# Other rooms for a few tiles of a hybrid decoder block: right halves of rows for w_up's first results, the scores' tile for every fifth gate

## The chip, the cores and the metric

The kernel runs on one core of one Trainium2 chip. Its time is device microseconds (us) of one launch; the median of three runs stands for a version. The profile is of one further execution, whose own time stands beside its span below.

Engines as the profile names them: PE is TensorE (matmuls; PEld is its weight load), DVE is VectorE, ACT is ScalarE, POOL is GpSimd, SP is the engine that here issues most DMAs (SPq its queue). L12 is line 12 of the kernel before; lines of the changed kernel are one or two higher behind the edits.

## The reference, cut to what matters

One decoder block on 1024 tokens of width 1024, all in float32:

```python
proj = x @ w_in                       # -> q, f, i, og, pool_v, gate_a, gate_b
a = HGRN2(q, f, i), per-head RMSNorm, * sigmoid(og), @ w_a
b = per-group linear w_pool of (causal_mean(pool_v) - pool_v), * pool_scale
mix = (sigmoid(gate_a) * a + sigmoid(gate_b) * b) @ w_out
x = LN(alpha * x + mix)
x = LN(alpha * x + relu(x @ w_up)**2 @ w_down)
```

## The kernel before, in words

Each float32 product is three matmuls: an operand is split into a high and a low part (ACT casts the high part, L133 for activations and L279 for weights; DVE subtracts for the low part, L134 and L280), and PE adds high·high (L238), high·low (L240) and low·high (L241) in one PSUM bank. Each large product is done as seven block products of a Strassen-like scheme instead of eight. `pair` (L330 is its adding, L326 its copying out of PSUM) is one such unit: seven products p1 to p7, each of 12 matmuls of 128x512, with sums of weight blocks on DVE (L335 to L367) and three or four results that are first parked in an SBUF tile (`rooms`).

The stages, in order: proj; a recurrence over 8 heads, whose steps (`turns`) are put between proj's products; the pooling's linear `w_pool` (`pool_products`), put between the products of the last two `gates`; w_a; w_out with the first LN; w_up in 16 units of 256 columns, whose results go to DRAM; w_down; the last LN.

Two places matter here.

**The gates of w_pool.** `pool_products` makes 16 small products of six matmuls (L115 to L117) into two PSUM banks of the tag `tr`. For 14 of them a tile of the ring `f` (four rooms) is first loaded from DRAM with a sigmoid gate (SP, L929, `f<-gb`), DVE multiplies it by the product (L936), and SP writes it back to DRAM (L937, `pb<-f`). A room can be loaded again when its write has landed; a bank can be used again when DVE has read it. SP issues its DMAs in a fixed order, so a load that waits holds those behind it. The recurrence's own tile for scores, `att` (512 columns), is read last by the matmuls of L1184, before these gates begin.

**The start of w_up.** `first_normed` and `second_tokens` make the seven token operands s3, a22, s2, s1, s4 on DVE and ACT while the first three units (`pairs[0]`, `pairs[1]`, `third`) multiply with those that are ready; `run_second` writes this order down: products 3 of both pairs, the third unit's first, products 4 and 5 of both pairs, the third unit's second, products 6 and 7. A unit's results ask for tiles with `c_tile`: it takes one from the list `spare` if there is any, and else one of the rings `ca` (4 rooms), `up` (4) and `wq` (2) in the turn ca, up, ca, up, wq, counted by `n_c`. Some rooms of ca and wq are still held by the normed right halves of the tokens (`xt[1]`, four tiles, which end as the operand s4). A tile of a ring is given to the next who asks when its last reader is done; where that is late, ACT's copy out of PSUM is late, and with it the next product into that bank. The rows `r[4]` to `r[7]` (1024 columns) are normed rows of the first LN: their left halves hold the third unit's weights from then on, their right halves are transposed into the operand a22 and then idle. `spare` gets these halves and the four tiles of `xt[2]` only before `third[2:]`.

The scheduler orders instructions of different engines by priorities; the order on each engine is fixed when the kernel is built.

Of the kernel before, what the change touches and what calls it, by code (L numbers as in the profile page):

```python
# [22 lines left out]
HALF = 512  # L23
CH = HALF // P
# [29 lines left out]
def tile_hybrid_block(  # L54
# [36 lines left out]
    def nm(s):  # L91
        seq[0] += 1
        return f"{s}_{seq[0]}"
# [7 lines left out]
    def ps_tile(tag="pj", bufs=4):  # L101
        if tag == "hg":
            hg_tags.append(hg_tags.pop(0))
            tag, bufs = hg_tags[-1], 1
        return pp.tile([P, HALF], F32, tag=tag, name=nm("ps_" + tag), bufs=bufs)

    def f(t):
        return t.bitcast(F32)
# [17 lines left out]
    def split(src, tile_of):  # L126
        hi, lo = tile_of(), tile_of()
        A.copy(hi, src)
        V.tensor_sub(lo, src, f(hi))
        return hi, lo  # L130
# [32 lines left out]
    r = [None] * 8  # L163
# [4 lines left out]
    @contextmanager  # L168
    def behind_parts(name):

        with tc.issue_after(made_last[name]), tc.issue_after(made_hi[name]):
            yield
# [13 lines left out]
    xt = [[None] * CH for _ in range(3)]  # L186
# [24 lines left out]
    def second_tokens(name, *tags, normal=False):  # L211
        a11, a12, s = xt
        turned = []
        for kp in range(CH):
            if name in ("s3", "a22"):
                ps, done = transposed(r[CH:], HALF if name == "a22" else 0, kp, tags[kp % len(tags)])
                turned.append(done)
                if normal:
                    t = s[kp] if name == "s3" else half_act()
                    normed(t, ps, kp + CH * (name == "a22"))  # L220
                    ps = t
            if name == "s3":
                V.tensor_sub(s[kp], a11[kp], ps)
            elif name == "s1":
                V.tensor_add(a11[kp], s[kp], a11[kp])
            elif name == "s4":
                V.tensor_sub(a12[kp], a12[kp], s[kp])
            in_parts(name, kp, dict(s3=s, s2=s, s1=a11, s4=a12)[name][kp] if name != "a22" else ps)
            if name == "a22":
                V.tensor_sub(s[kp], ps, s[kp])  # L230
        return turned
# [51 lines left out]
    @contextmanager  # L283
    def behind_weight(n=-1):

        with tc.issue_after(hi_of[n]), tc.issue_after(lo_of[n]):
            yield
# [11 lines left out]
    n_c = [0]  # L299
# [7 lines left out]
    spare = []  # L307
# [122 lines left out]
    def run(*pairs, made=(), behind=()):  # L430

        for i, steps in enumerate(zip(*pairs)):
            made_now = list(made[i]) if made else []
            if made_now:
                made_now.pop(0)()
            with tc.issue_after(made_last[behind[i]]) if behind and behind[i] else nullcontext():
                ws = [{operand: operand() for operand in operands} for operands, _ in steps]
            for n in range(len(ws[0])):
                if made_now:
                    made_now.pop(0)()  # L440
                for w, (_, products) in zip(ws, steps):
                    operand, product = products[n]
                    product(w[operand])
                    next(turning[0], None)
# [19 lines left out]
    def run_second(pairs, third):  # L464

        def later(name, tag=None, after=None, added=False):
            def made():
                with tc.issue_after(last_add[0] if added else made_last[after]) if after else nullcontext():
                    second_tokens(name, tag, normal=True)
            return made  # L470

        made = (
            (lambda: None, later("a22", "tr")), (later("s2", after="s3"),), (later("s1", after="s2"),),
            (lambda: None, later("s4", after="s1")), (),
        )
        behind = (None, "s3", None, None, None)
        run(*(p[2 : 3] for p in pairs), made=made, behind=behind)
        with behind_parts("s3"):
            run(third[:1])
        run(*(p[3 : 5] for p in pairs), made=made[1:], behind=behind[1:])  # L480
        run(third[1:2])
        run(*(p[5 :] for p in pairs), made=made[3:], behind=behind[3:])

    def row_tile():
        return w_tile().rearrange("p k c -> p (k c)")
# [6 lines left out]
    ca = ctx.enter_context(tc.tile_pool(name="ca", bufs=4, reuse_waits="tile"))  # L492
    wq = w_scope.enter_context(tc.tile_pool(name="wq", bufs=1, side="right", reuse_waits="tile"))
# [258 lines left out]
    def loaded(src, tile_of):  # L752
        t = tile_of()
        nc.sync.dma_start(out=t, in_=src)
        return t
# [31 lines left out]
    with tc.tile_pool(name="tmp", bufs=1, side="right", reuse_waits="tile") as tmp:  # L787
# [3 lines left out]
        att = hgp.tile([P, CH, P], F32, name="att")  # L791
# [11 lines left out]
        def tt(tag, dtype=F32):  # L803
            pool = tmp if tag in ("q", "f", "og", "v") else hgp
            return pool.tile([P, HALF], dtype, tag=tag, name=nm(tag), bufs=RINGS.get(tag, 1))
# [77 lines left out]
        def pool_products():  # L883

            def ring(*tags):
                tags = list(tags)
                def tile(dtype=F32):
                    tags.append(tags.pop(0))
                    return tt(tags[-1], dtype)
                return tile  # L890

            pod_tile, w_tiles = ring("tA", "tA", "st", "st", "tH", "tH"), ring("tD", "tE", "tF", "og")

            def wide(t):
                return t.rearrange("p (k c) -> p k c", c=2 * P)

            def load(g, u):
                raw = None
                if not u:
                    raw = loaded(w_pool[g].rearrange("(k p) c -> p k c", p=P), lambda: wide(tt("tC")))  # L900
                return raw, [loaded(pod[2 * g + i][u], pod_tile) for i in range(2)]

            def parts(g, u, raw, pods):
                with behind_weight():
                    if raw is not None:
                        w_parts[g] = split(raw, lambda: wide(w_tiles(F32R)))
                    made = []
                    for t in pods:
                        hi, lo = row_tile(), row_tile()
                        pool_parts[:] = A.copy(hi, t).ins, V.tensor_sub(lo, t, f(hi)).ins  # L910
                        made.append((hi, lo))
                    return made

            w_parts = {}
            todo = [(g, u) for g in range(CH) for u in range(2)]
            soon = [load(*todo[0]), load(*todo[1])]
            pl = parts(*todo[0], *soon.pop(0))
            yield
            for n, (g, u) in enumerate(todo):
                if n + 2 < len(todo):  # L920
                    soon.append(load(*todo[n + 2]))
                wh, wl = w_parts[g]
                for i in (0, 1) if g < CH - 1 else (1, 0):
                    w = slice(i * P, (i + 1) * P)
                    j = 2 * g + i
                    final = j == KT - 1
                    t = tt("v") if final else tt("f")
                    if not final:
                        nc.sync.dma_start(out=t, in_=gbd[j][u])  # L929
                    ps = ps_tile("tr", 2)  # L930
                    mm3(ps, [(wh[:, c, w], wl[:, c, w], *pl[c]) for c in range(2)])
                    if final:
                        held[u] = t
                        A.activation(t, ps, AF.Copy, scale=pscale[:, j : j + 1])
                    else:
                        V.scalar_tensor_tensor(t, ps, pscale[:, j : j + 1], t, ALU.mult, ALU.mult)  # L936
                        nc.sync.dma_start(out=pbd[j][u], in_=t)  # L937
                    if i == (1 if g < CH - 1 else 0) and soon:
                        pl = parts(*todo[n + 1], *soon.pop(0))
                    yield  # L940
# [519 lines left out]
    r = [None] * 8  # L1460
# [39 lines left out]
    with tc.tile_pool(name="up", bufs=1, side="right", reuse_waits="tile") as up:  # L1500
        n_c[0] = 0

        def c_wide(short=None):
            n_c[0] += 1
            pool, n = ((ca, 4), (up, 4), (ca, 4), (up, 4), (wq, 2))[n_c[0] % 5]
            return pool.tile([P, HALF + 2 * HALO], F32, tag="c", name=nm("c"), bufs=n)[:, : HALO + HALF]

        def up_raw_tile():
# [52 lines left out]
            run(pairs[1][:1])  # L1561
        run_second(pairs, third)

        spare[:] = [*xt[2], *(r[t][:, HALF:] for t in range(CH, 8))]
        run(third[2:])
        spare.clear()
        rows_scope.close()
# [140 lines left out]
    for b in range(NBLK):  # L1708
# [3 lines left out]
        if last:  # L1712

            for ring in (dh, dw):
                t = fw.tile([P, M, 2, HALF], F32R, tag="draw", name=nm("dx"), bufs=2)
                ring[:0] = [(t[:, n], t[:, n + 1]) for n in (0, 2)]
        for i, (name, slot, chain, fresh, (u, nh)) in enumerate(steps):
# [13 lines left out]
            for c in range(CH):  # L1731
                t = u * CH + c
# [49 lines left out]
```

## Time and profile before

| | us |
|---|---|
| runs | 1443.65, 1442.93, 1444.0; median 1443.65 |
| profiled execution, its own time | 1443.23 |
| its span, first to last instruction | 1441.5 |
| PE busy | 1417.4 (98% of the span) |
| DVE busy | 1141.2 (79%) |
| ACT busy | 772.9 (54%) |
| POOL busy | 129.6 (9%) |

PE is busy for 98% of the span, so a change is worth what it takes from PE's waits or from PE's own work. A busy matmul is not a fast one: a 128x512 matmul starts about 0.23 us behind the one before it at the full granted clock and 0.42 us behind it at half, and both count as busy. So two views are read together: who waited for whom, and the granted clock (PEclk) stretch by stretch.

### The profile page before, as it was taken

To read this page: it belongs to the slowest core of one execution; us is meant where nothing else is said; L and a number is where in the kernel's file an instruction comes from. 1 tells how busy PE (TensorE), PEld (TensorE's weight loads), DVE (VectorE), ACT (ScalarE), POOL (GpSimd) and SP (SyncE) were. 2 spreads that over 40 slices of the span, in tenths; PEclk is the share of its full clock that TensorE was granted. 3 is DMA by queue.
4 is the path that set the end of the run, shared out by engine and by line. 5 is a ranking of instruction groups with operands and counts; after the bars stand their busy time and mean duration, and the time that the engine had idled before them with its cause. 6 is when DMAs were issued, how large, how long until landed. Compare 5 with 4: busy or idle time off the path is not lost.

```text
span 1441.5 us, 21398 instructions
## 1 busy us (share of the span) xinstructions
PE 1417.4 (98%) x7451; PEld 1172.5 (81%) x7451; DVE 1141.2 (79%) x1928; ACT 772.9 (54%) x1411; POOL 129.6 (9%) x354
## 2 busy tenths in 40 slices
PE   8999999999999999999999989999999999999997
PEld 7878888888888888878888768788888888888886
DVE  5968887897798796679996896966666887777978
ACT  5445566666656656455445664555556443433534
POOL 0023011111212110100110000100000100000000
PEclk9999999999999999999999999999999999999999
DMA  7285254444444546798762327954456874444422
GB/s 270 62 276 176 85 133 156 120 115 151 112 119 132 147 123 190 229 323 289 252 225 82 120 67 242 320 174 161 144 177 249 288 246 150 149 140 168 130 73 117
DMA packets 193036, 248.12 MB, mean 172 GB/s; under 512 B 13552, under 2 KB 112160, under 8 KB 192928
## 3 DMA queue, kind: packets, MB, share of 16 engines
q1 hardware_dynamic: 179312, 208.84, 43.7%
q0 software_dynamic: 11648, 33.56, 8.6%
q10 hardware_dynamic: 1968, 4.35, 1.0%
q8 instruction: 58, 0.95, 0.3%
q14 instruction: 50, 0.41, 0.1%
HBM read 161.24 MB, written 85.46 MB: 171 GB/s over the span
## 4 chain that ended last, share of the span: by engine, by line
PE 87%; DVE 5%; DMA 4%; ACT 2%; issue 1%; SPq 0%; DVEq 0%; ACTq 0%
PE ps_pj L238 15%; PE ps_pj L240 15%; PE ps_pj L241 15%; PE ps_pj L1661 4%; PE ps_pj L1660 4%; PE ps_pj L1659 4%; PE ps_tr L1661 2%; PE ps_tr L1660 2%; PE ps_tr L1659 2%; DMA act<-in_w_in_dram 1%; PE ps_sc L238 1%; PE ps_sc L240 1%; PE ps_sc L241 1%; PE ps_hg L241 1%; PE ps_hg L240 1%; PE ps_hg L238 1%
## 5 line engine op out<-in xcount | busy, mean ns | idle before, releaser
L238 PE MATMUL ps_pj<-act,w 128*128 128x512 f32 x1068 | 421.0, 394 | 5.6 <-ACT w L279 2.1
L240 PE MATMUL ps_pj<-act,w 128*128 128x512 f32 x1068 | 415.9, 390 | 0.0
L241 PE MATMUL ps_pj<-act,w 128*128 128x512 f32 x1068 | 414.8, 390 | 0.5 <-DVE w L280 0.5
L279 ACT CAST w<-raw 128x512 fp32r<-128x512 f32 x303 | 187.5, 621 | 237.1 <-PE ps_pj L240 169.5
L280 DVE TENSOR_TENSOR w<-raw,w 128x512 fp32r<-128x512 f32 x303 | 206.5, 685 | 78.8 <-ACT w L279 77.4
L238 PEld LDWEIGHTS ps_pj<-act,w 128*128 128x128 f32 x1068 | 200.9, 188 | 52.5 <-ACT c L326 4.2
L241 PEld LDWEIGHTS ps_pj<-act,w 128*128 128x128 f32 x1068 | 200.6, 188 | 43.6 <-DVE w L280 1.3
L240 PEld LDWEIGHTS ps_pj<-act,w 128*128 128x128 f32 x1068 | 200.8, 188 | 40.4 <-DVE act L134 0.3
L1621 ACT CAST act<-act 128x1024 fp32r<-128x1024 f32 x66 | 67.1, 1050 | 108.3 <-issue 35.0
L1622 DVE TENSOR_TENSOR act<-act,act 128x1024 fp32r<-128x1024 f32 x66 | 79.4, 1219 | 17.6 <-ACT act L1621 17.6
L1661 PE MATMUL ps_pj<-act,act 128*128 128x512 f32 x240 | 93.0, 389 | 0.0
L1660 PE MATMUL ps_pj<-act,act 128*128 128x512 f32 x240 | 93.0, 389 | 0.0
L1659 PE MATMUL ps_pj<-act,act 128*128 128x512 f32 x240 | 92.5, 389 | 0.0
L330 DVE TENSOR_TENSOR c<-c,ps_pj 128x512 f32<-128x512 f32 x91 | 62.1, 682 | 33.6 <-PE ps_pj L241 29.7
L326 ACT COPY c<-ps_pj 128x512 f32<-128x512 f32 x92 | 53.6, 582 | 7.0 <-DMA v<-c 4.8
L1660 PEld LDWEIGHTS ps_pj<-act,act 128*128 128x128 f32 x240 | 45.0, 188 | 9.4
L1661 PEld LDWEIGHTS ps_pj<-act,act 128*128 128x128 f32 x240 | 45.0, 188 | 9.3
L1659 PEld LDWEIGHTS ps_pj<-act,act 128*128 128x128 f32 x240 | 45.0, 188 | 9.3
L335 DVE TENSOR_TENSOR raw<-raw,raw 128x512 f32<-128x512 f32 x43 | 29.6, 688 | 28.2 <-DMA raw<-in_w_in_dram 17.8
L1512 ACT ACTIVATE c<-c 128x512 f32<-128x512 f32 x46 | 29.1, 632 | 30.6 <-DVE c L330 30.5
L1513 ACT ACTIVATE c<-c 128x512 f32<-128x512 f32 x61 | 38.5, 633 | 1.5
L782 POOL DMA_DIRECT2D s<-og x28 | 24.8, 1159 | 133.8 <-DVE og L1208 133.8
(496 smaller groups left out, 2756.8 us busy)
## 6 DMA issues: line engine op xcount, KB each, us to landing
h<-c SPq DMA_DIRECT2D x106, 256.0 KB, 2.9
raw<-in_w_in_dram SPq DMA_DIRECT2D x100, 256.0 KB, 3.2
act<-h SPq DMA_DIRECT2D x78, 256.0 KB, 3.0
draw<-in_w_down_dram SPq DMA_DIRECT2D x16, 1024.0 KB, 8.1
raw<-in_w_up_dram SPq DMA_DIRECT2D x56, 256.0 KB, 3.0
hf<-h SPq DMA_DIRECT2D x34, 256.0 KB, 2.9
s<-og POOLq DMA_DIRECT2D x28, 256.0 KB, 6.3
v<-v SPq DMA_DIRECT2D x16, 256.0 KB, 4.6
```

Of the source, the lines that this page charges most:

```text
L238: PE.matmul(ps, wh[:, k], th, start=first and k == 0, stop=False, skip_group_check=True)
L240: PE.matmul(ps, wh[:, k], tl, start=False, stop=False, skip_group_check=True)
L241: last_product[0] = PE.matmul(ps, wl[:, k], th, start=False, stop=k == CH - 1, skip_group_check=True).ins
L279: hi_of.append(A.copy(hi, src).ins)
L280: lo_of.append(V.tensor_sub(lo, src, f(hi)).ins)
L326: noted(A.copy(t, ps))
L330: last_add[0] = V.tensor_add(t, t, ps).ins
L1621: A.copy(hi, src)
L1622: V.tensor_sub(lo, src, f(hi))
L1659: PE.matmul(ps, hh[:, w], wh, start=fresh and n == 0, stop=False, skip_group_check=True)
L1660: PE.matmul(ps, hh[:, w], wl, start=False, stop=False, skip_group_check=True)
L1661: PE.matmul(ps, hl[:, w], wh, start=False, stop=n == M - 1, skip_group_check=True)
```

## The change

Three edits. In `run_second` the right halves of rows 4 to 7 go into `spare` as soon as products 3 of both pairs (and with them the transposes into a22) are written down, so the next four tiles asked for are r[7], r[6], r[5], r[4]; the four tiles of xt[2] are added to the list before `third[2:]`. The first six tiles of w_up come by a turn of their own, up, ca, up, up, ca, up; the fourth was wq's. And every fifth room asked for by a gate is the scores' tile `att`, so gates 5 and 10 of 16 use it.

```diff
         run(*(p[2 : 3] for p in pairs), made=made, behind=behind)
+        spare[:] = [r[t][:, HALF:] for t in range(CH, 8)]
         with behind_parts("s3"):
             run(third[:1])
...
-            w_parts = {}
+            w_parts, rooms_used = {}, [0]
...
-                    t = tt("v") if final else tt("f")
+                    rooms_used[0] += 1
+                    t = tt("v") if final else tt("f") if rooms_used[0] % 5 else att.rearrange("p c q -> p (c q)")
...
-            pool, n = ((ca, 4), (up, 4), (ca, 4), (up, 4), (wq, 2))[n_c[0] % 5]
+            pool, n = ((ca, 4), (up, 4), (ca, 4), (up, 4), (wq, 2))[n_c[0] % 5 if n_c[0] > 6 else (0, 1, 0, 1, 1, 0, 1)[n_c[0]]]
...
-        spare[:] = [*xt[2], *(r[t][:, HALF:] for t in range(CH, 8))]
+        spare.extend(xt[2])
         run(third[2:])
```

No instruction of PE, ACT or POOL is added or taken away; their order changes from the start of w_up on.

**SP among the gates of w_pool.** Names: gb4_0 is the gate of column block 4 and token half 0, pb the written product; `raw` are weights of w_a. Gates are made in the order 2_0, 3_0, 2_1, 3_1, 4_0, 5_0, 4_1, 5_1 from the fifth on. Before:

```order
L937 DMA pb2_0_1014<-f_1286_6922 128x512
L929 DMA f_1299_6982<-gb3_1_985 128x512
L754 DMA st_1333_7093<-po6_1_1007 128x512
L937 DMA pb3_0_1016<-f_1288_6933 128x512
L754 DMA st_1334_7095<-po7_1_1009 128x512
L929 DMA f_1321_7043<-gb4_0_986 128x512
L873 DMA gb6_0_990<-c_1294_6964 128x512
L253 DMA raw_1369_7282<-in_w_a_dram 128x4x128
L937 DMA pb2_1_1015<-f_1297_6971 128x512
L929 DMA f_1323_7054<-gb5_0_988 128x512
L937 DMA pb3_1_1017<-f_1299_6982 128x512
L929 DMA f_1335_7097<-gb4_1_987 128x512
```

The same place with the change:

```order
L939 DMA pb2_0_1014<-att_1067 128x512
L931 DMA f_1320_7042<-gb4_0_986 128x512
L755 DMA st_1331_7091<-po6_1_1007 128x512
L939 DMA pb3_0_1016<-f_1287_6932 128x512
L755 DMA st_1332_7093<-po7_1_1009 128x512
L931 DMA att_1067<-gb5_0_988 128x512
L874 DMA gb6_0_990<-c_1293_6963 128x512
L253 DMA raw_1367_7280<-in_w_a_dram 128x4x128
L939 DMA pb2_1_1015<-f_1296_6970 128x512
L931 DMA f_1333_7095<-gb4_1_987 128x512
L939 DMA pb3_1_1017<-f_1298_6981 128x512
L931 DMA f_1335_7106<-gb5_1_989 128x512
```

Each load stands one load earlier: where gate 8 (gb3_1) was loaded stands gate 9 (gb4_0), and so on. Gate 5 (gb2_0) is loaded into att far ahead of this, between the loads st<-po0_1 and tA<-po1_0 of SP.

**ACT and PE at the start of w_up.** ps_hg and ps_sc are the PSUM banks of products 7 and 4 of the two pairs, ps_tr banks of transposes, c and r tiles the parked results. On ACT the copy out of ps_sc stood here before, the first of these rows being the operand s4's last cast:

```order
L133 CAST act_1772_9366<-c_1671_8820 128x512
L1512 ACTIVATE c_1743_9218<-c_1743_9218 128x512
L1513 ACTIVATE c_1743_9218<-c_1743_9218 128x512
L1512 ACTIVATE c_1760_9304<-c_1760_9304 128x512
L1513 ACTIVATE c_1760_9304<-c_1760_9304 128x512
L326 COPY c_1739_9199<-ps_sc_1738_9183 128x512
```

and stands here now, two rows behind the copy out of ps_hg:

```order
L326 COPY c_1735_9179<-ps_hg_1734_9163 128x512
L279 CAST w_1745_9231<-raw_1691_8983 128x512
L326 COPY c_1737_9197<-ps_sc_1736_9181 128x512
L133 CAST act_1731_9149<-act_1730_9147 128x512
L198 ACTIVATE act_1730_9147<-ps_tr_1732_9153,prm_126 128x512
```

On PE the second pair's product 4 (12 matmuls into ps_sc) stood behind all of products 6 before:

```order
L241 MATMUL ps_pj_1707_9034<-act_1755_9281,w_1766_9345 128x512
L238 MATMUL ps_pj_1742_9205<-act_1744_9220,w_1786_9468 128x512
L240 MATMUL ps_pj_1742_9205<-act_1744_9220,w_1786_9468 128x512
L238 MATMUL ps_sc_1738_9183<-act_1728_9130,w_1750_9240 128x512
L240 MATMUL ps_sc_1738_9183<-act_1728_9130,w_1750_9240 128x512
L241 MATMUL ps_sc_1738_9183<-act_1728_9130,w_1751_9241 128x512
```

and begins now among the first pair's product 4, some 60 matmuls earlier:

```order
L238 MATMUL ps_hg_1734_9163<-act_1726_9128,w_1745_9231 128x512
L240 MATMUL ps_hg_1734_9163<-act_1726_9128,w_1745_9231 128x512
L238 MATMUL ps_sc_1736_9181<-act_1726_9128,w_1747_9237 128x512
L240 MATMUL ps_sc_1736_9181<-act_1726_9128,w_1747_9237 128x512
L241 MATMUL ps_hg_1734_9163<-act_1726_9128,w_1746_9232 128x512
L238 MATMUL ps_hg_1734_9163<-act_1728_9138,w_1745_9231 128x512
```

**DVE behind the operand s4.** Here DVE adds products out of PSUM (L330), which frees banks for the next products, and makes the low parts of s4 (L134 from c tiles). Before, the first pair's ps_pj_1707 was added behind two of the four low parts:

```order
L330 TENSOR_TENSOR c_1743_9218<-c_1743_9218,ps_tr_1764_9330 128x512
L280 TENSOR_TENSOR w_1768_9350<-raw_1723_9117,w_1767_9349 128x512
L280 TENSOR_TENSOR w_1774_9400<-raw_1696_8990,w_1773_9399 128x512
L330 TENSOR_TENSOR c_1760_9304<-c_1760_9304,ps_hg_1736_9165 128x512
L280 TENSOR_TENSOR w_1776_9404<-raw_1698_8994,w_1775_9403 128x512
L134 TENSOR_TENSOR act_1769_9354<-c_1668_8817,act_1769_9354 128x512
L134 TENSOR_TENSOR act_1770_9358<-c_1669_8818,act_1770_9358 128x512
L330 TENSOR_TENSOR c_1737_9181<-c_1737_9181,ps_pj_1707_9034 128x512
```

Now its twin, ps_pj_1705, is added behind all four and behind the sum L335, whose inputs are unit 3's loads:

```order
L330 TENSOR_TENSOR r_1624_8507<-r_1624_8507,ps_tr_1759_9325 128x512
L280 TENSOR_TENSOR w_1781_9463<-r_1620_8475,w_1780_9462 128x512
L134 TENSOR_TENSOR act_1764_9349<-c_1666_8815,act_1764_9349 128x512
L134 TENSOR_TENSOR act_1765_9353<-c_1667_8816,act_1765_9353 128x512
L134 TENSOR_TENSOR act_1766_9357<-c_1668_8817,act_1766_9357 128x512
L335 TENSOR_TENSOR raw_1795_9579<-raw_1797_9582,raw_1796_9580 128x512
L134 TENSOR_TENSOR act_1767_9361<-c_1669_8818,act_1767_9361 128x512
L330 TENSOR_TENSOR c_1735_9179<-c_1735_9179,ps_pj_1705_9032 128x512
```

## The prediction

> **What bounds the kernel.** First the page's busy times, then who waited for whom on PE, then the granted clock around the longest waits.
>
> ```profile
> span 1441.5 us, 21398 instructions
> PE 1417.4 (98%) x7451; PEld 1172.5 (81%) x7451; DVE 1141.2 (79%) x1928; ACT 772.9 (54%) x1411; POOL 129.6 (9%) x354
> ```
>
> PE is idle for 24.1 us of the span, so no change that leaves PE's work alone can bring much more. The waits of PE:
>
> ```profile
> PE ps_sc L238 <- ACT c L326: 3.2, 1, 3.2
> PE ps_pj L238 <- ACT c L326: 2.0, 3, 1.0
> PE ps_tr L115 <- DVE f L936: 2.0, 1, 2.0
> ```
>
> Two of the longest single waits are the places of this change: 3.2 us for ACT's copy out of ps_sc (start of w_up) and 2.0 us for DVE's read of a gate's bank. Stretches around both, and three wider ones used further down (us; busy time of PE, PEld, DVE, ACT, POOL with counts; granted clock, DMA share, GB/s):
>
> ```profile
> 622.20:626.00 3.80, 3.80 (x10) 2.99 (x11) 3.09 (x5) 1.76 (x3) 0.23 (x1) 0.55 0.95 319
> 852.20:857.50 5.30, 5.27 (x12) 4.13 (x13) 5.24 (x9) 1.89 (x4) 0.00 (x0) 0.50 0.27 102
> 817.60:839.30 21.70, 19.67 (x88) 14.38 (x87) 21.37 (x35) 17.64 (x32) 0.00 (x0) 1.00 0.31 94
> 839.30:857.40 18.10, 13.77 (x48) 10.25 (x47) 18.10 (x31) 12.05 (x22) 0.00 (x0) 0.83 0.22 74
> 610.00:660.00 50.00, 48.04 (x204) 39.06 (x203) 39.87 (x65) 31.16 (x56) 2.73 (x5) 0.97 1.00 335
> ```
>
> Behind each of the two waits the clock is granted at about half for 3.8 and 5.3 us, and there PE counts as busy while it works at half pace. So each wait costs nearly twice its length. The third row holds a wait of 1.10 us (832.10, below) at a clock of 1.00: what halves it lies between 1.1 and 2.0 us.
>
> [...]
>
> **Edit 1, the gates.** Ten rows of PE, DVE and SP, and the landing time of the loads:
>
> ```profile
> 608.70 0.32 SPq L929 DMA_DIRECT2D f<-gb  x1
> 613.44 0.67 SPq L937 DMA_DIRECT2D pb<-f  x1
> 615.42 0.32 SPq L929 DMA_DIRECT2D f<-gb  x1
> 615.76 0.39 PE L117 MATMUL ps_tr<-w,og 128*128 128x512 f32 x1
> 619.85 0.39 PE L117 MATMUL ps_tr<-w,tE 128*128 128x512 f32 x1
> 620.78 0.32 SPq L929 DMA_DIRECT2D f<-gb  x1
> 621.39 0.75 DVE L936 SCALAR_TENSOR_TENSOR f<-ps_tr,prm,f 128x512 f32<-128x512 f32 x1 [4.79 <-DMA f<-gb]
> 622.19 0.61 PE L115 MATMUL ps_tr<-w,tD 128*128 128x512 f32 x1 [1.96 <-DVE f L936]
> 645.63 0.68 DVE L280 TENSOR_TENSOR w<-raw,w 128x512 fp32r<-128x512 f32 x1
> 647.68 0.39 PE L241 MATMUL ps_pj<-act,w 128*128 128x512 f32 x1
> DMA to landing us min/median/max: 3.6/3.8/3.9
> ```
>
> Gate 8's product ended at 616.2, but its load, issued at 615.42, had DVE wait until 621.39; gate 10 needs gate 8's bank and began at 622.19 where its turn was 619.85 + 0.23 = 620.08. That is 2.1 us, and nine steps at half clock cost 0.2 each more: 1.7. Together 3.8.
>
> With gate 5 in att, each load moves to the SP row of the one before: gate 8's to 608.70. Even 5.9 us later, as here, it lands at 614.6, ahead of its product: the wait goes. Next late is gate 10, which reads att: that load waits for the write of 613.44, as the one at 620.78 does now, and stands in the same row. Landing 3.8 to 5.9 later, plus 0.75 of DVE, frees its bank at 625.4 to 627.4; PE wants it for gate 12 at 620.1 + 1.4 (gate 10) + 2.7 (a product of 12) + 1.4 (gate 11) = 625.6. New wait 0 to 1.8; I take 0.5. Behind the waiting load on SP stand gate 6's last load, a weight of w_a and gate 7's write, the same as before.
>
> What the shift is worth is decided later: from 610 to 660 the DMA share is 1.00, so data come little earlier than now. PE's closest margin there is 647.68 against a low part ready at 646.31: 1.4 us. Adding 0.8 for one 256 KB load drawn forward at 335 GB/s gives 2.2; with what the waits leave (3.8 - 0.5 = 3.3) as the upper end I take **2.3**, between 0 (DMA full) and 3.8.
>
> The first load into att is new ahead of other loads on SP and waits for att's last reader:
>
> ```profile
> L1184 PE MATMUL ps_hg<-v,att x128: 270/275/275, 162.2 to 568.4; 128*128 128x128 f32 x128
> 569.00 0.32 SPq L754 DMA_DIRECT2D tA<-po  x1
> ```
>
> The reader ends at 568.7, and the next DMA of SP left at 569.00 anyway: no cost (at worst one issue, 0.3 us, on loads that are not waited for by PE).
>
> **Edits 2 and 3, the start of w_up.** Rows of ACT, PE, DVE and SP:
>
> ```profile
> 827.14 0.61 ACT L326 COPY c<-ps_hg 128x512 f32<-128x512 f32 x1
> 851.61 0.57 ACT L326 COPY c<-ps_sc 128x512 f32<-128x512 f32 x1
> 830.60 0.40 PE L240 MATMUL ps_hg<-act,w 128*128 128x512 f32 x1
> 832.10 0.50 PE L238 MATMUL ps_pj<-act,w 128*128 128x512 f32 x1 [1.10 <-ACT w L279]
> 837.03 0.50 PE L241 MATMUL ps_pj<-act,w 128*128 128x512 f32 x1 [0.47 <-DVE w L280]
> 844.77 0.50 PE L238 MATMUL ps_pj<-act,w 128*128 128x512 f32 x1 [0.64 <-ACT c L326]
> 848.34 0.50 PE L238 MATMUL ps_pj<-act,w 128*128 128x512 f32 x1 [0.54 <-ACT w L279]
> 852.23 0.79 PE L238 MATMUL ps_sc<-act,w 128*128 128x512 f32 x1 [3.16 <-ACT c L326]
> 831.48 0.68 DVE L280 TENSOR_TENSOR w<-raw,w 128x512 fp32r<-128x512 f32 x1
> 838.71 0.68 DVE L134 TENSOR_TENSOR act<-r,act 128x512 fp32r<-128x512 f32 x1
> 839.31 2.49 DVE L225 TENSOR_TENSOR r<-r 128x512 f32<-128x512 f32 x4
> 842.43 6.99 SPq L253 DMA_DIRECT2D raw<-in_w_up_dram  x2
> 870.89 0.39 PE L238 MATMUL ps_pj<-act,w 128*128 128x512 f32 x1
> ```
>
> The copy out of ps_sc came 24 us behind its twin out of ps_hg, since its room was still s4's. In PE's order 132 matmuls lie from just before 830.60 (at 830.37) to 870.89, the same work in both kernels: 40.5 us, of which 132 x 0.227 = 30.0 are work at full pace. So 10.6 us are lost there.
>
> Now the copy follows the twin by two rows (828.1), which pushes ACT's next casts by its 0.5 us, and the 12 matmuls of ps_sc fill holes earlier. What is left, going along PE with DVE's and ACT's rows as they stand:
> - behind 830.60 two of the moved matmuls run, then the low part of 831.48 is waited for, ready at 832.16: 0.85 us;
> - the ten others put PE 2.3 us later, so the waits at 837.03, 844.77 and 848.34, whose releasers keep their times, are gone;
> - about 850.8 two waits for the third unit's next weights (ACT cast, DVE low part): 0.2 and 0.6;
> - then the add of ps_pj_1705 (last row of the part on the change). DVE has no pause here: the row 839.30:857.40 is busy for 18.10 of 18.10, four in 2.41 us (839.31 to the next at 841.72), 0.603 each. In the new order L225 takes the slot at 838.71, and this add is 27 rows behind: it starts at 838.71 + 27 x 0.603 = 855.0 and is done at 855.7. PE arrives at 854.5: a wait of 1.2 us, nearest to the 1.10 that left the clock at 1.00;
> - restarts, 0.11 each (0.34 instead of 0.23 behind 848.34), four: 0.45.
>
> Sum 3.3, so **10.6 - 3.3 = 7.3** come back. The bounds: 0 (the hole reappears in full) to 10.6. Unit 3's first weights are not late: SP's last load of the row 842.43 left at 849.0, as then.
>
> Rooms behind that: both kernels take ten rooms in turn, so each is asked for again after ten tiles, one and a half units; I count nothing.
>
> **Sum.** 1443.23 - 2.3 - 7.3 = 1433.6 for an execution like the profiled one, which lies 0.4 below the median of 1443.65; I say **1433.7**.
>
> **Rivals.**
> 1. The DMA queues keep the gates' shift: for it the share of 1.00; against it PE's margin of 1.4. Only the w_up part stays: 1443.2 - 7.3 = 1435.9.
> 2. DVE is held in front of that add: L335, now two rows ahead of it, needs the load of 849.0. It is due at DVE at 853.8; a load of 6 us, as this one,
>
> ```profile
> 881.23 6.01 DMA raw<-in_w_up_dram
> ```
>
> lands at 855.05, holds DVE 1.25 and makes PE's wait 2.45, long enough for half clock (2.6): 1433.6 + 3.9 = 1437.5. Against it the DMA share of 0.22 there.
> 3. The half clock is not the waits' doing and stays: 1.7 + 2.6 come back, 1437.9. [...]
> 4. It does not do what it says: the holes close at the two places and open as long behind them, since DVE is full from 839 to 857 and the DMAs from 610 to 660. What is left of 9.6 is under 2.9: 1441 to 1445.
> 5. Slower: rooms. Now all eight spare halves are used up before unit 3, and its copies go to rooms just written, while the DMAs are full again (880 to 930):
>
> ```profile
> 880.00:930.00 50.00, 48.58 (x212) 39.17 (x211) 40.96 (x69) 24.17 (x45) 7.86 (x15) 1.00 0.90 296
> ```
>
> If a copy (L326) there waits for a write of h as the one at 851.61 did for its room, it costs 3.2 + 2.7 = 5.9; from the second such copy the gain is gone, and two in place of none give 1433.6 + 11.8 = 1445.4. Against it: ten tiles, 27 us, lie between two uses of a room, and PE's only wait there is 1.0.
>
> **How the numbers follow.** Forecast 0.52 (1431 to 1436), rival 1 0.12, rival 2 0.11, rival 3 0.09, rival 4 0.09, rival 5 0.07. About 0.2% (2.9 us) is what a measurement here tells from no change. Faster than that: forecast and rivals 1 to 3, 0.84; within: rival 4, 0.09; slower: 0.07. The range runs from 1430.0 (the bounds 3.8 and 10.6 nearly in full) to 1441.0, the edge of rival 4; that leaves out 0.16.
>
> **What would show it.** Right: no wait at L115 over 1 us near 620 and clock 1.00 there; ACT's copy out of ps_sc within 2 us of ps_hg's; PE's waits from 830 to 860 under 1.3 each, the last for DVE L330; the same work done 7 us sooner. Wrong: half-clock stretches without a wait of 2 us before them, a wait on ACT L326 or on L335's load, or PE's later waits on h writes.

## The result, and the profile after

The changed kernel takes 1433.92 us (median of four runs, 1432.04 to 1434.64), the kernel before 1443.51 beside it: ratio 0.9932, interval 0.9914 to 0.9949. In six runs of a later occasion it took 1433.76 against 1442.0, ratio 0.9942 (0.9924 to 0.9959). The forecast was 1433.7.

The profiled execution took 1433.87 us, 9.4 less than the one before. Its span and PE's busy time:

```profile
span 1432.2 us, 21387 instructions
PE 1414.3 (99%) x7451; PEld 1170.9 (82%) x7451; DVE 1140.3 (80%) x1928; ACT 772.7 (54%) x1411; POOL 129.4 (9%) x354
```

The span fell by 9.3 us, PE's busy time by 3.1, with the same 7451 matmuls. So 6.2 us are idle time of PE that went, and 3.1 are work that now runs at a faster clock (mean granted 0.998, before 0.995).

Whom PE waited for, longest first (the wait on POOL is in the first 2 us):

```profile
PE ps_hg L507 <- POOL ident masks.py:199: 1.8, 1, 1.8
PE ps_pj L238 <- DVE c L330: 1.7, 2, 1.0
PE ps_hg L241 <- DVE w L280: 0.7, 1, 0.7
```

The waits on ACT c L326 (3.2) and on DVE f L936 (2.0) are gone; the longest behind the first microseconds is 1.0, for the add L330 that the forecast named.

The two places as stretches (us; busy time of PE, PEld, DVE, ACT, POOL; granted clock, DMA share, GB/s):

```profile
619.00:626.00 7.00, 7.00 (x33) 5.79 (x32) 3.17 (x6) 3.40 (x6) 0.38 (x1) 1.00 1.04 358
827.67:871.00 43.33, 41.44 (x178) 32.83 (x177) 40.89 (x68) 30.82 (x55) 1.63 (x3) 1.00 0.46 152
```

Among the gates PE is busy without a hole at clock 1.00, although the DMA share is still 1. At the start of w_up the clock stays at 1.00 too, and 1.9 us in 43 are idle.

The rows of SP, ACT and PE there, and two waits further on:

```profile
608.64 0.32 SPq L931 DMA_DIRECT2D f<-gb  x1
619.18 0.32 SPq L931 DMA_DIRECT2D att<-gb  x1
824.39 0.61 ACT L326 COPY c<-ps_hg 128x512 f32<-128x512 f32 x1
825.38 0.63 ACT L326 COPY c<-ps_sc 128x512 f32<-128x512 f32 x1
829.48 0.50 PE L241 MATMUL ps_hg<-act,w 128*128 128x512 f32 x1 [0.74 <-DVE w L280]
852.95 0.50 PE L238 MATMUL ps_pj<-act,w 128*128 128x512 f32 x1 [1.04 <-DVE c L330]
919.48 0.50 PE L241 MATMUL ps_sc<-act,w 128*128 128x512 f32 x1 [0.46 <-DVE w L280]
1141.25 0.50 PE L1662 MATMUL ps_pj<-act,act 128*128 128x512 f32 x1 [0.63 <-DVE act L1624]
```

The copy out of ps_sc follows its twin by 1.0 us where it came 24 us behind. PE's two waits of the stretch are the longer two of the four that the forecast had put there. For its other two, on the third unit's weights, PE lost 0.25 and 0.19 us (848.59 and 849.34, start to start) where 0.2 and 0.6 were put. The last two rows are new small waits.

**Where the 9.4 us came from.** Two waits that both kernels have, in rows of before and then of after, cut the execution into parts:

```profile
494.31 0.50 PE L238 MATMUL ps_pj<-act,w 128*128 128x512 f32 x1 [0.62 <-DVE c L330]
806.46 0.50 PE L238 MATMUL ps_pj<-act,w 128*128 128x512 f32 x1 [0.41 <-DVE r L207]
```

```profile
494.96 0.50 PE L238 MATMUL ps_pj<-act,w 128*128 128x512 f32 x1 [0.64 <-DVE c L330]
803.67 0.50 PE L238 MATMUL ps_pj<-act,w 128*128 128x512 f32 x1 [0.42 <-DVE r L207]
```

Up to the first, after is 0.65 late, in code that the change leaves alone. Between them before took 312.15 and after 308.71: 3.4 for the gates. At the start of w_up, in the stretch that the forecast had counted at 10.6 us lost, after loses 3.2 (start to start of matmuls, beyond 0.227 each): 7.4. Behind it before lost 2.2 (890, 908, 912; the first two are waits on ACT) and after 2.7 (919, 1140, 1153): 0.5 against. Together 3.4 + 7.4 - 0.65 - 0.5 = 9.6, of 9.4.

### The profile page after: what moved, and what is told of

It reads as the page before. It is cut to its first block, busy times and chain, and to the rows that moved or that the text cites. A ratio compares the mean times of both kernels' runs of the same rounds, so it can differ in the third digit from the quotient of the medians.

```text
span 1432.2 us, 21387 instructions
## 1 busy us (share of the span) xinstructions
PE 1414.3 (99%) x7451; PEld 1170.9 (82%) x7451; DVE 1140.3 (80%) x1928; ACT 772.7 (54%) x1411; POOL 129.4 (9%) x354
## 4 chain that ended last, share of the span: by engine, by line
PE 88%; DVE 6%; DMA 3%; issue 2%; ACT 1%; SPq 0%; POOL 0%; DVEq 0%; POOLq 0%; ACTq 0%
PE ps_pj L238 15%; PE ps_pj L241 15%; PE ps_pj L240 15%; PE ps_pj L1662 4%; PE ps_pj L1663 4%; PE ps_pj L1661 4%; PE ps_tr L1663 1%; PE ps_tr L1661 1%; PE ps_tr L1662 1%; PE ps_sc L241 1%; PE ps_hg L241 1%; PE ps_sc L238 1%; PE ps_sc L240 1%; PE ps_hg L238 1%; PE ps_hg L240 1%
## 5 line engine op out<-in xcount | busy, mean ns | idle before, releaser
L279 ACT CAST w<-raw 128x512 fp32r<-128x512 f32 x303 | 187.7, 622 | 232.0 <-PE ps_pj L240 158.1
L330 DVE TENSOR_TENSOR c<-c,ps_pj 128x512 f32<-128x512 f32 x91 | 62.1, 684 | 31.6 <-PE ps_pj L241 28.0
L326 ACT COPY c<-ps_pj 128x512 f32<-128x512 f32 x89 | 51.8, 582 | 8.1 <-PE ps_pj L241 4.0
L1662 PEld LDWEIGHTS ps_pj<-act,act 128*128 128x128 f32 x240 | 45.0, 188 | 10.6 <-DVE act L1624 1.3
L335 DVE TENSOR_TENSOR raw<-raw,raw 128x512 f32<-128x512 f32 x43 | 29.7, 691 | 29.1 <-DMA raw<-in_w_in_dram 19.6
L1514 ACT ACTIVATE c<-c 128x512 f32<-128x512 f32 x43 | 27.2, 633 | 20.3 <-DVE c L330 20.3
L1515 ACT ACTIVATE c<-c 128x512 f32<-128x512 f32 x57 | 35.8, 632 | 1.3
```

What stands on the lines that cost most here:

```text
L279: hi_of.append(A.copy(hi, src).ins)
L326: noted(A.copy(t, ps))
L330: last_add[0] = V.tensor_add(t, t, ps).ins
L1662: PE.matmul(ps, hh[:, w], wl, start=False, stop=False, skip_group_check=True)
```

## The experiments

Twelve kernels ran, four on each of three occasions. Each ratio is to runs of the kernel before on the same chip. There before spread from 1438.2 to 1448.6 in 58 runs, so times decide only between steps of some 2.5 us, and the traces decide the rest.

To compare traces I use one measure, **lost at w_up**: the time beyond 0.227 us from one matmul's start to the next, where that is over 0.02 us, between 7.5 and 52 us behind PE's wait on ACT act L133 (at 820.65 in before), which all kernels share.

| kernel | lost at w_up, us | ratio to before |
|---|---|---|
| before; before_again; e1_gates | 10.5; 9.4; 9.4 | 1; 1.000; 0.999 |
| e4_halves | 5.1 | 0.9964 |
| e3_turn; gates_turn | 3.9; 5.5 | 0.9963; 0.9947 |
| after; after_again; e2_start | 3.1; 3.1; 3.1 | 0.9932; 0.9942; 0.9959 |
| add_first; rows_later | 1.7; 1.7 | 0.9947; 0.9946 |

**The gates alone.**

```diff
-                    t = tt("v") if final else tt("f")
+                    rooms_used[0] += 1
+                    t = tt("v") if final else tt("f") if rooms_used[0] % 5 else att.rearrange("p c q -> p (c q)")
```

> The gates' edit alone: gates 5 and 10 use att, the start of w_up is as before. Theory (each wait costs its length and the half clock behind it, and the two places are independent): no wait on DVE f L936 near 620, granted clock 1.00 from 619 to 630, 3.3 to 3.8 us less than before, 1440.0, ratio 0.9975; the wait of 3.2 us on ACT c L326 and the half clock behind it stay at the start of w_up, some 3.4 us earlier. Rival (the DMA queues hold the gates' part back, and the whole gain comes from w_up): the wait near 620 goes, but PE waits as long for weights before 660, 1443.5, ratio 1.000.

Measured: 1440.06 against 1442.09, ratio 0.9990 (0.9974 to 1.0007): 2.0 us, which the times tell neither from the 3.3 to 3.8 expected nor from nothing. PE has no wait at L115 near 620, and one of 0.49 us for a weight's low part at 645.28, a small part of what the rival had put there. The wait at ps_sc stays, and the clock behind it falls 0.6 us late (row, then stretches):

```profile
850.03 0.50 PE L238 MATMUL ps_sc<-act,w 128*128 128x512 f32 x1 [3.16 <-ACT c L326]
849.80:850.80 1.00, 0.77 (x3) 0.68 (x4) 1.00 (x3) 1.00 (x3) 0.00 (x0) 0.90 0.09 31
850.80:854.00 3.20, 3.20 (x8) 2.43 (x8) 3.20 (x7) 0.93 (x2) 0.00 (x0) 0.50 0.24 87
854.00:858.00 4.00, 4.00 (x19) 3.31 (x18) 3.14 (x6) 1.90 (x3) 0.00 (x0) 1.00 0.52 197
```

The wait went as expected. That the gain looks smaller than in the pair of profiles has its reason in before_again, below.

**The start of w_up alone** (turn and early halves, the gates as before; diff as in the change).

> The two edits at the start of w_up alone (turn and early halves), gates as before. Theory: the wait of 2.0 us on DVE f L936 and its half clock stay; the stretch of 132 matmuls at the start of w_up loses 3.2 us where it lost 10.6, so 7.4 us less, less up to 1 us that small waits behind take: 1436.1 to 1437.1, ratio 0.9953, and the gains of the two parts add up to that of the change within 0.5 us. Rival (the parts need each other: without the gates' shift weights or DVE come later at w_up): under 5 us, above 1438.5.

Measured: 1436.51, ratio 0.9959 (0.9944 to 0.9975). Lost at w_up 3.1, as with all edits: this part needs nothing from the gates. The two parts' ratios multiply to 0.9949, and the change has 0.9932 and 0.9942: within the intervals they add up. The expected wait of 2.0 near 620 was not there in this execution; PE waited 0.55 and 0.41 instead.

**Each of the two edits at w_up alone.** The turn:

```diff
-            pool, n = ((ca, 4), (up, 4), (ca, 4), (up, 4), (wq, 2))[n_c[0] % 5]
+            pool, n = ((ca, 4), (up, 4), (ca, 4), (up, 4), (wq, 2))[n_c[0] % 5 if n_c[0] > 6 else (0, 1, 0, 1, 1, 0, 1)[n_c[0]]]
```

> Only the turn of w_up's first six tiles; the halves of rows 4 to 7 are handed out late, as before. Theory: the copy out of ps_sc moves to two rows behind its twin and the wait of 3.2 us with its half clock goes, but the third unit's copy out of ps_pj now asks for a room that s4's source still holds and stands at ACT's row 886, so a new wait on ACT c L326 shows at a ps_pj matmul near 850: 3 to 6 us less than before, 1437.5 to 1440.5. Rival (the halves do nothing, the turn is all): as both together, 1436.1 to 1437.1 and no such wait.

and the halves:

```diff
         run(*(p[2 : 3] for p in pairs), made=made, behind=behind)
+        spare[:] = [r[t][:, HALF:] for t in range(CH, 8)]
...
-        spare[:] = [*xt[2], *(r[t][:, HALF:] for t in range(CH, 8))]
+        spare.extend(xt[2])
```

> Only the early halves; the fourth tile of w_up is wq's as before. Theory: the copy out of ps_sc is still held by s4's source, the wait of 3.2 us on ACT c L326 and the half clock stay near 852: 0 to 1 us less than before, 1442.5 to 1443.5, ratio 0.9995. Rival (any relief of rooms opens the place): 4 us or more less, under 1439.5.

Measured: the turn 1437.48, ratio 0.9963 (0.9949 to 0.9976); the halves 1436.59, ratio 0.9964 (0.9948 to 0.9981). The first came at the edge of the expected range, though not by the expected wait: PE's waits there are for DVE, none for a held copy.

```profile
847.74 0.47 PE L238 MATMUL ps_hg<-act,w 128*128 128x512 f32 x1 [1.25 <-DVE c L330]
849.45 0.50 PE L241 MATMUL ps_pj<-act,w 128*128 128x512 f32 x1 [1.01 <-DVE w L280]
```

The second is a plain miss: I expected nothing and it has nearly all of the turn's gain, as the rival said. ACT's copies and PE's wait with the halves alone:

```profile
845.80 1.06 ACT L326 COPY r<-ps_pj 128x512 f32<-128x512 f32 x2
853.85 0.58 ACT L326 COPY c<-ps_sc 128x512 f32<-128x512 f32 x1
854.00 0.50 PE L238 MATMUL ps_hg<-act,w 128*128 128x512 f32 x1 [0.48 <-ACT w L279]
```

The copy out of ps_sc is as late as ever (853.85), yet PE does not wait for it. In the kernel before two copies stood one behind the other on ACT, ps_sc's at 851.61 and one out of ps_pj at 852.08, both for held rooms. With a free half the one out of ps_pj is made some 7 us before the other (the second of the two at 845.80), and PE has the third unit's products to do until ps_sc's copy is made: from 844.72 it runs 30 matmuls into ps_pj, and ps_sc's follow at 854.57, where the kernel before ran 18 and then stood at ps_sc. So two holds closed on PE at once, and opening either one lets it go on.

**A second profile of before**, with no edit.

> The kernel before once more, for a second profile of it. Theory (a wait of about 2 to 3 us is followed by half clock in some executions and not in others, and the gates' wait changes with the DMA's landing): PE's wait on ACT c L326 near 852 is 3.1 to 3.2 us again; half clock behind it or not; the wait on DVE f L936 near 620 lies between 0.5 and 2.0 us. Rival (the first profile is what every execution does): waits of 1.96 and 3.16 us, half clock behind both, 3.8 and 2.6 us lost by it as before. Ratio 1.000.

Measured: ratio 1.000 (0.9984 to 1.0015). Rows of PE, and the stretch behind the second:

```profile
620.32 0.50 PE L115 MATMUL ps_tr<-w,tD 128*128 128x512 f32 x1 [1.47 <-DVE f L936]
849.24 0.50 PE L238 MATMUL ps_sc<-act,w 128*128 128x512 f32 x1 [3.15 <-ACT c L326]
888.67 0.50 PE L238 MATMUL ps_pj<-act,w 128*128 128x512 f32 x1 [2.59 <-ACT c L326]
850.20:853.50 3.30, 3.30 (x10) 2.53 (x9) 3.30 (x7) 0.75 (x2) 0.00 (x0) 0.50 0.23 84
888.60:894.00 5.40, 5.33 (x23) 4.43 (x24) 3.19 (x5) 2.17 (x5) 0.00 (x0) 1.00 1.01 315
```

The wait at ps_sc is the same to 0.01 us, since it hangs on the order of instructions; the half clock behind it now costs 1.6 us and not 2.8. The gates' wait, which hangs on a DMA's landing, is 1.47 and has no half clock behind it; in the profiles of e3_turn and e4_halves it is 0.91 and 1.37. So the first profile of before had the gates at their dearest. All fourteen profiles (before, after and the twelve of this section) have the same order on PE up to the start of w_up, so one stretch can be compared in all: from the matmul that starts at 617.13 in before to the wait on DVE r L207. It takes 189.3 us in the first profile of before, 187.0 to 187.7 in the other four with the old rooms, and 185.5 to 186.3 in the nine with att. By the means (187.3 and 185.7) the gates bring 1.7 us where no half clock falls among them, and 3.4 in the first pair.

**How long a wait brings the half clock.** One, two or four DVE subtractions into a dead tile, in front of the add that PE waits for at 853:

```diff
+            if name == "s4" and kp in (2, 3):
+                V.tensor_sub(s[kp], a12[kp], f(xp[name][kp][:, 0]))
```

(kp in (3,) for one, (0, 1, 2, 3) for four.) The condition also holds in the first stage's s4, where I had not meant it: each kernel has as many extra subtractions there.

> The changed kernel with one more DVE subtraction (0.60 us, into a tile that nobody reads) in front of the add that PE waits for at the start of w_up: PE's wait on DVE c L330 near 853 grows from 1.05 to 1.65 us. Theory (a wait of more than 1.1 to 2.0 us is followed by half clock for some 5 us): 0.6 us more than the changed kernel, 3.2 us more if 1.65 is past the threshold; the mean granted clock of its runs then falls by 0.002. Rival (the half clock needs over 3 us of idle PE): 0.6 us more, clock as in the changed kernel.

> Two more DVE subtractions in front of the same add: PE's wait 2.25 us. Theory (half clock behind waits of 2 us): 1.2 us for the wait and 2.6 for the half clock behind it, 3.8 us more than the changed kernel, mean clock of the runs lower by 0.002. Rival (the half clock needs over 3 us of idle PE, as behind the wait of 3.16 us of the kernel before, whose profile would then have had its other half clock stretch for another reason): 1.2 us more, clock as in the changed kernel.

> Four more DVE subtractions in front of the same add: PE's wait 3.46 us. Theory and the rival of 3 us alike: 2.4 us for the wait and 2.6 for the half clock, 5.0 us more than the changed kernel, mean clock lower by 0.002 in nearly all runs. Second rival (the half clock comes by chance, as the gates-only kernel had a wait of 3.16 us and none behind it): 2.4 us more, and the clocks of the runs spread as those of the changed kernel.

> The changed kernel once more, beside the three with a longer wait. Theory: 6 to 10 us less than before, ratio 0.993 to 0.996, no half clock stretch in the profile, mean clocks of the runs 0.998 to 0.999 where the kernel before has 0.996 to 0.997. Rival (the first comparison was a lucky chip): ratio 0.996 or above, as the start of w_up alone gave.

Measured: 1434.91, 1435.49 and 1441.93, beside 1433.76 for the changed kernel again, whose ratio is as expected; its profile has one stretch of half clock all the same, behind a wait of 1.64 us at 489, far ahead of the change. The times of low1 (ratio 0.9949, 0.9934 to 0.9964) and low2 (0.9951, 0.9935 to 0.9968) cannot be told from the changed kernel's: the 1.7 us of low2 lie between its rival's 1.2 and the 3.8 of the theory, and the subtractions in the first stage mix in. So the traces decide. PE's waits came as ordered: 1.65, 2.21 and 3.46. A row and a stretch of low1:

```profile
850.15 0.50 PE L240 MATMUL ps_pj<-act,w 128*128 128x512 f32 x1 [1.65 <-DVE c L332]
849.85:853.26 3.41, 3.11 (x14) 2.57 (x15) 3.41 (x7) 3.23 (x7) 0.00 (x0) 1.00 0.15 55
```

of low2:

```profile
853.35 0.50 PE L240 MATMUL ps_pj<-act,w 128*128 128x512 f32 x1 [2.21 <-DVE c L332]
853.30:854.60 1.30, 1.25 (x5) 1.05 (x6) 1.30 (x3) 1.30 (x4) 0.00 (x0) 1.00 0.00 0
854.60:858.00 3.40, 3.40 (x10) 2.62 (x9) 3.40 (x6) 2.77 (x6) 0.00 (x0) 0.51 0.61 229
858.00:861.00 3.00, 3.00 (x15) 2.47 (x13) 3.00 (x6) 1.61 (x3) 0.54 (x1) 0.99 0.95 304
```

and of low4, with a wait of its first stage:

```profile
134.25 0.57 PE L240 MATMUL ps_pj<-act,w 128*128 128x512 f32 x1 [3.06 <-DVE c L332]
859.56 0.79 PE L240 MATMUL ps_pj<-act,w 128*128 128x512 f32 x1 [3.46 <-DVE c L332]
859.50:864.90 5.40, 5.34 (x13) 4.17 (x14) 5.40 (x11) 3.69 (x8) 0.00 (x0) 0.50 0.51 192
```

Behind 1.65 the clock stays at 1.00; behind 2.21 it is half, 1.3 us late and for 3.4 us; behind 3.46 it is half at once, for 5.4. Lost at w_up: 3.7, 5.9, 8.0 against 3.1, so the third costs 4.9, the 5.0 expected, and the second 2.8 of the 3.8 expected. The further 3 us of low4's time come from the first stage, as far as its one profile shows: that took 6.3 us longer there than in the changed kernel's, with PE's wait of 3.06 and 1.7 us lost to half clock behind it. The rival that asks for 3 us of idle PE falls with the trace of low2, and the one of pure chance with low4 and the kernels with the wait of 3.16, which had it every time.

**Without the early halves.** The changed kernel less the halves (the diff of the halves, undone).

> The changed kernel without the early halves (gates and turn only). Theory, amended by the runs with one edit alone (turn alone lost 3.3 us in the stretch at the start of w_up, halves alone 5.1, both 3.0, neither 8.8 to 10.3): the halves add 0.3 us at most once the turn is there: within 1 us of the changed kernel, ratio to before 0.993 to 0.996. Rival (the halves are needed with the gates' shift): 2 us or more slower than the changed kernel.

(The figures in it are of a slightly shorter stretch than the table's.) Measured: 1434.46, ratio 0.9947 (0.9926 to 0.9968), within 1 us of the changed kernel. Its two waits at w_up and the stretch behind:

```profile
846.15 0.47 PE L238 MATMUL ps_hg<-act,w 128*128 128x512 f32 x1 [1.25 <-DVE c L330]
847.86 0.79 PE L241 MATMUL ps_pj<-act,w 128*128 128x512 f32 x1 [1.01 <-DVE w L280]
847.80:851.00 3.20, 3.14 (x7) 2.48 (x8) 3.20 (x7) 2.69 (x5) 0.00 (x0) 0.51 0.21 82
```

The same two waits as in e3_turn; there the clock stayed at 1.00, here it is half. Two waits of 1.25 and 1.01 us, 0.7 us of work apart, were followed here by half clock, as the one of 2.21 in low2 was, and there they were not. The last section shows what the two executions differ in.

**The adds first**, an attempt at a faster version:

```diff
-            (lambda: None, later("s4", after="s1")), (),
+            (lambda: None, later("s4", after="s1")), (made_lows,),
...
+        def made_lows():
+            with tc.issue_after(last_add[0]):
+                for t, src in lows:
+                    V.tensor_sub(t[:, 1], src, f(t[:, 0]))
```

> The changed kernel with the low parts of operand s4 written down behind the two adds of products 5 instead of ahead of them; the same instructions. Theory: DVE adds ps_pj_1705 some 2.4 us earlier, PE's wait on DVE c L330 near 853 (1.05 us, 1.2 with the step in front) goes, and no wait for a low part takes its place, since PE needs one low part per three matmuls (0.68 us) and DVE makes one in 0.60: 1.3 us less lost in the stretch of the start of w_up, 1432.5. Rival: the low parts become late in turn, a wait on DVE act near 853 of up to 1.2 us, no gain.

and, on top of it, the residual rows held back:

```diff
-                V.tensor_mul(y[:, w], y[:, w], g1[:, w])
+                with behind_add():
+                    V.tensor_mul(y[:, w], y[:, w], g1[:, w])
```

> As the run with the adds first, and the residual rows' multiplications on DVE are held behind the last add of the unit that they are written behind. In four of six profiles of kernels with the changed start of w_up, DVE stood 3 us waiting for a residual row's load at 914 to 921 and PE then 0.5 to 2.0 us for a low part behind it. Theory: no wait on DVE w L280 near 920, 0.5 to 2 us less than with the adds first alone. Rival: the rows' work comes later into busier places, and PE waits on DVE elsewhere in w_up: no gain or a loss.

Measured: 1434.29 and 1434.33, ratios 0.9947 (0.9927 to 0.9966) and 0.9946 (0.9929 to 0.9963). In the first PE's wait at 853 is gone and one stretch of 27 us there loses 0.5:

```profile
829.42 0.50 PE L246 MATMUL ps_hg<-act,w 128*128 128x512 f32 x1 [0.74 <-DVE w L285]
829.00:856.00 27.00, 26.50 (x114) 21.10 (x114) 27.00 (x46) 18.62 (x34) 0.00 (x0) 1.00 0.21 69
```

Lost at w_up falls from 3.1 to 1.7, as expected, and the wait of 1.05 is shown to be DVE's order. In the time it cannot be told from the changed kernel. The residual rows stay open: neither kernel had the wait near 920. In six of the ten profiles with the turn PE waited there 0.5 to 2.0 us and DVE 1.1 to 3.4 before it for a row's load (less than the 3 us throughout that I had written). The second kernel had 2.07 us on ACT w at 878 instead.

## Why the prediction was right, by its steps

- **What bounds it** held: PE's work is untouched, and the gain is PE's two waits and the clock behind them.
- **The gates, 2.3** (between 0 and 3.8): 3.4 against the profile it was made for, mis-sized downwards. The new wait at gate 12 that I took at 0.5 did not come, and the full DMA queues kept nothing back, so rival 1 fell for this pair. But the term is not steady: the old wait is 0.5 to 2.0 with the DMA's landing, and in executions without half clock there the gain is some 1.7.
- **The start of w_up, 7.3**: 7.4, and what was left, 3.3, is 3.2. The waits came where the forecast walked them along PE: 0.85 before the low part (0.74 idle, 0.90 start to start), 1.2 for the add of ps_pj_1705 (1.04 idle, 1.2 start to start), the three of 837, 844 and 848 gone. Of the small terms one was off: the second wait on weights, put at 0.6, was 0.19. Against the second profile of before and that of e1_gates, which lost 9.4 each, this part is worth 6.3.
- **Unit 3's load** (rival 2) did not hold DVE: with the earlier start of w_up it left SP at 839.7 to 840.7, and L335 ran at 850.98 without a wait.
- **"What halves it lies between 1.1 and 2.0 us"** is the step that failed as it was put. One wait's length does not decide. Waits of 1.62 to 2.67 were followed by half clock six times in eleven (1.64 in after_again, 1.96 in before and 2.21 in low2 were; 1.65 in low1, 2.07 in rows_later and 2.59 in before_again were not), two of 1.25 and 1.01 together once in two (in gates_turn, not in e3_turn), those over 3.0 five times in five (3.16 in before and e1_gates, 3.15 in before_again, 3.06 and 3.46 in low4), single ones of up to 1.58 never. What goes with the half clock in the fourteen profiles is how much idle time of PE falls into the 3.41 us ahead of it: 1.96 and 2.58 us in before, 2.25 in gates_turn, where e3_turn with 1.25 and 1.01 and after with at most 1.04 kept the full clock (last section). That this is what decides is an estimate from these profiles. The price is 1.6 to 2.8 us each: the wait of 3.16 us cost 2.8 more in the first profile, "nearly twice its length", and 1.6 more, half its length, in the second. Rival 3, no link to the waits, fell: every stretch of half clock between the first 40 us and the last matmuls, twelve in fourteen profiles, begins within 2 us of the end of such a wait (in before 0.2 us after the one of 1.96 and 1.1 us before the end of the one of 3.16, in low2 1.3 us after, in after_again 1.7).
- **Rivals 4 and 5** had a little truth in sum and none in kind: 2.7 us of small waits lie behind 871 where 2.2 lay before, for weights, residual rows and w_down's parts (DVE), not for writes of h.
- **Which edit does it** the forecast left as one sum. The runs show that turn and halves do the same work twice: alone they lose 3.9 and 5.1 at w_up, together 3.1.

That the forecast came within 0.3 us of the median owes something to chance: the first profile of before (1443.23) lay above the median of that kernel's later runs (1442.0 to 1442.1), with the gates at their dearest, and I had sized them low. For a usual execution the traces give less than the forecast's 9.6: 1.7 for the gates and 6.3 for w_up, less the 0.5 behind it, 7.5 us, where the later times give 8.2.

## What to carry to other kernels

When PE stands still because a copy out of PSUM has no room, look for the other copies queued behind it on the same engine: here two holds closed at once, and opening either one was enough (lost at w_up: 3.9 and 5.1 us instead of 10.5). The wait that hangs on instruction order repeated to 0.01 us (3.16, 3.15 and 3.16 in before, before_again and e1_gates), the one that hangs on a DMA's landing did not (1.96, 1.47, 0.91 and 1.37 in before, before_again, e3_turn and e4_halves); take the first at its face value and the second as a range, from more than one profile if there is one. Walk the instructions of the new order along the engines with the old durations: here that put both remaining waits within 0.2 us.

## What the runs showed of the hardware

The half clock comes in pieces. In the granted clock of the traces ten of the twelve stretches last 3.41 us (in before 622.43 to 625.84) and two 6.83, twice that (in before 851.12 to 857.95). In those two (the first profile of before and low4) PE was still idle for the first 1.1 and 1.4 us, so that its matmuls ran at half for 5.7 and 5.4. The other ten began between 0.2 us before PE resumed and 1.7 us after. Behind the wait of 3.15 to 3.16 us at ps_sc the clock fell 1.1 us before PE resumed in before, and 0.6 and 0.9 us after in e1_gates and before_again.

In the trace of before these changes lie on one grid. Counted from the fall at 622.43, the return at 625.84, the fall at 851.12, the return at 857.95 and the fall behind the last matmul, at 1438.22, come 1.0, 67.0, 69.0 and 239.0 times 3.413 us later. No run shows what sets it. Laid out in such steps, each of the two stretches of before stands between the step ahead of it and the one behind:

```profile
619.02:622.43 3.41, 1.45 (x7) 0.91 (x6) 1.04 (x2) 0.77 (x2) 0.55 (x1) 1.00 1.08 353
622.43:625.84 3.41, 3.41 (x9) 2.63 (x9) 2.75 (x5) 1.76 (x3) 0.07 (x1) 0.50 0.91 325
625.84:629.26 3.42, 3.42 (x16) 2.82 (x16) 1.79 (x4) 0.62 (x1) 0.47 (x1) 1.00 0.89 283
847.71:851.12 3.41, 0.83 (x3) 0.30 (x2) 3.41 (x7) 3.35 (x7) 0.00 (x0) 1.00 0.21 63
851.12:854.54 3.42, 2.31 (x6) 1.83 (x7) 3.42 (x7) 2.80 (x5) 0.00 (x0) 0.50 0.26 96
854.54:857.95 3.41, 3.41 (x10) 2.64 (x9) 3.09 (x6) 0.62 (x1) 0.00 (x0) 0.50 0.49 184
857.95:861.36 3.41, 3.41 (x16) 2.82 (x15) 1.79 (x3) 1.26 (x2) 0.00 (x0) 1.00 0.33 124
```

Here are the two steps of gates_turn around the fall of its clock, then the two of e3_turn that hold the same two waits (its steps are counted back from the half clock behind its last matmul, at 1428.13):

```profile
844.47:847.88 3.41, 1.16 (x5) 0.33 (x4) 3.41 (x7) 3.08 (x6) 0.00 (x0) 1.00 0.02 5
847.90:851.27 3.37, 3.37 (x8) 2.69 (x9) 3.37 (x6) 2.59 (x5) 0.00 (x0) 0.50 0.20 78
844.45:847.86 3.41, 2.16 (x11) 1.50 (x10) 3.41 (x7) 2.72 (x5) 0.00 (x0) 1.00 0.00 0
847.86:851.27 3.41, 2.40 (x10) 1.68 (x11) 3.41 (x7) 3.12 (x7) 0.00 (x0) 1.00 0.02 5
```

In gates_turn both waits lie in one step, PE is idle for 2.25 us of it, and the clock is half in the next. In e3_turn an edge parts them, 1.25 and 1.01 us are idle, and the clock stays. The fourteen profiles have some 5600 such steps between the first 40 us and the last matmuls. The twelve with half clock behind them, where it was full before, hold 1.64 to 3.06 us of idle PE (1.96 and 2.58 in before); of the others one holds 1.93 us and none of the rest more than 1.62 (at most 1.11 in before and 1.04 in after, whose steps are counted back from 1427.56, where the clock falls behind its last matmul). The two of 1.64 lie at 487 and 488, among the recurrence's small matmuls. So no one figure parts the two kinds: 1.64 us was followed by half clock and 1.93 us was not. The ends of matmuls are modelled in the profile, so these figures are only as sharp as they are. The half clock went on for a second step where its first held 1.1 and 1.4 us of idle PE (before and low4) and ended where it held 0.23 or less (0.00 behind 622.43 in before).
